# Three matmul operands at other places in SBUF: the mixer's output, the gates' second operand, the values' activations

## The chip, the core and the metric

The kernel runs on one core of one Trainium2 chip. The metric is the device time of the program on that core in microseconds (us). The time of a kernel is the median of its runs.

## What is computed

One layer of an encoder over 256 tokens (`S`) of width 2048 (`D`), all in float32. Cut to what matters here:

```
mod = silu(c) @ w_ada + b_ada            # six vectors: shift, scale, gate, twice
h   = x * (1 + scale1) + shift1
mix = concat([ssd(h @ w_in), shortconv(h @ w_in)]) @ w_out     # 4096 columns of mixer output
x   = layer_norm(alpha * x + gate1 * mix)
h   = x * (1 + scale2) + shift2
q   = h @ w_query                        # 8 heads, product keys, top 16 of 128*128 experts
act = gelu(expert_u @ h) * gate          # 16384 experts as 128 chunks of 128
x   = layer_norm(alpha * x + gate2 * (act @ expert_v))
```

## The kernel before

Everything runs with features or experts on the 128 partitions. Weights stream in as blocks of 128x1024 floats (`raw`), and `wsplit` (L70 to L83) cuts each into a high and a low part, `hi` on ACT (L78) and `lo` on DVE (L81). A product is then three matmuls with float32r operands, written in `mm3` (L91 to L93): high weight with high activation, high with low, low with high. A matmul here has two operands in SBUF: the **weight** (the stationary one, 128 columns, loaded by an LDWEIGHTS ahead of it) and the **moving** one, which streams through. PE runs them in the order in which the program issues them; the profile shows the loads as the engine PEld.

In order of time, the stages and their matmuls are:

- `ps` and `ps_b` (`unit_b`), then `ps_in` (`inproj`): the input projection. The moving operand is `h2h` or `h2l`, 256 columns; the weight is `hi` or `lo`.
- `ps_o` (the loop over `d0, d1` after `out_chunk`): the output projection. The moving operand is the mixer's output, tiles `y` (`y_tiles`, L224 to L226; written in `rms` by `split`, L118 to L120). 3 x 512 = 1536 matmuls of 256 columns.
- `ps_q`: the queries, moving `h2h` and `h2l` again, and the top-16 search on DVE.
- `ps_u` (`act_chunk`, L821 to L826): the 128 chunks of `expert_u`, 48 matmuls each, moving `h2h` and `h2l`. In the first 64 chunks `proj` calls `step` twice a chunk, and each call puts one pair of **gate matmuls** (`ps_g`, L814, in `gates`) between two groups of 24 matmuls of `ps_u`. Their weight is `eq` (a comparison result of DVE, L803), their moving operand is `o2`, which ACT writes (L809). The results `ge` of these chunks go out to HBM (`gel_d`, L841) and come back in the second 64 chunks (L849).
- `ps_v` (`mm_v`, L874 to L881): act @ expert_v. Here the roles turn: the weight is the activation, `ah` or `al` (`a_pair`, L867 to L872), and the moving operand is the split block of `expert_v`, `hi` or `lo`, 512 columns. 3 x (992 + 32) = 3072 matmuls.

Which tile lies where in SBUF is set by the pools: tiles of a pool stand in the order in which they are first asked for, one after the other, and a pool that is opened with `side="right"` grows from the other end. The tiles of the change are in the pools `prm` (with `scb`, `par`, and ahead of `yp`, which holds `y`), `wk4a` (`eq`, `o2`, `ge`) and `wk5` (right side: `big5`, `g2b`, `st`, `ah`, `al`). The order of instructions is the program's own with some priorities; the change touches none of them.

Of the kernel before, what the change touches and what calls it, by code (L numbers as in the profile page):

```python
# [7 lines left out]
F32 = mybir.dt.float32  # L8
F32R = mybir.dt.float32r
# [9 lines left out]
P = 128  # L19
S = 256  # L20
D = 2048
ND = D // P
NE = 128
# [17 lines left out]
def layer_kernel(ctx, tc, I, out, dbg=None):  # L41
    nc = tc.nc
# [6 lines left out]
    def pool(stack, name, bufs=1, **kw):  # L49
        return stack.enter_context(tc.tile_pool(name=name, bufs=bufs, reuse_waits="tile", **kw))  # L50
# [169 lines left out]
    prm = pool(st2, "prm")  # L220
# [7 lines left out]
    scb = prm.tile([P, D], F32, name="scb")  # L228
    par = prm.tile([P, 194], F32, name="par")
    at = 0  # L230
# [564 lines left out]
    with ExitStack() as p4:  # L795
# [3 lines left out]
        def gates(q):  # L799

            eq = wk.tile([P, 2, 2, NE], F32R, name="eq", tag="eq")
            t0 = 2 * q
# [17 lines left out]

        def act_chunk(e2, wk, n, beside=None):  # L821
            ps = pu.tile([P, S], F32, name="ps_u", tag="pu")
            proj([ps], [I["expert_u"][e2]], *h2, ND, beside=beside)
            ge = wk.tile([P, S], F32, name="ge", tag="ge", bufs=n)
            other(ge, ps, AF.Gelu)
            return ge  # L826

        with ExitStack() as p4a:
            wk = pool(p4a, "wk4a", 2)
            pairs = (g for q in range(S // 2) for g in (gates(q),))  # L830
            g = next(pairs)
            next(g)

            def step():
                nonlocal g
                next(g, None)
                g = next(pairs, iter(()))
                next(g, None)

            for e2 in range(STAGE):  # L840
                nc.sync.dma_start(gel_d[e2], act_chunk(e2, wk, 1, step))  # L841
        wk = pool(p4, "wk4b")
# [13 lines left out]
    with ExitStack() as p5:  # L856
# [7 lines left out]
        g2b = wk.tile([P, D], F32, name="g2b")  # L864
        st = wk.tile([P, 2, 16], F32, name="st")

# [7 lines left out]
        def mm_v(tb, c, ah, al, vh, vl, lo, start, stop):  # L874

            ts = slice(tb * P, (tb + 1) * P)
            if not lo:
                T.matmul(banks[tb][c], ah[:, ts], vh, start=start, stop=False)  # L878
                T.matmul(banks[tb][c], al[:, ts], vh, start=False, stop=False)  # L879
            else:  # L880
                T.matmul(banks[tb][c], ah[:, ts], vl, start=False, stop=stop)  # L881


# [14 lines left out]
        for e2 in range(NE - LAST):  # L898
            if e2 % 2 == 0:
                ah, al = a_pair(e2)  # L900
            if e2 == FIRST:
# [133 lines left out]
```

## Time and profile before

| what | value |
|---|---|
| median of 3 runs | 2547.92 us |
| the 3 runs | 2544.36, 2547.92, 2559.14 us |
| the profiled execution, its own time | 2552.61 us |
| its span in the trace, first to last instruction | 2550.7 us |
| PE busy | 2424.6 us, 95% |
| DVE busy, ACT busy | 1862.2 us (73%), 1381.3 us (54%) |
| mean granted clock of PE | 0.984 |

The page's busy share of PE says that some matmul is in flight. It does not say how far apart they start. Matmuls overlap in the trace: a matmul of 256 columns is shown 0.28 us long, but the next one starts some 0.11 us after it. So the pace of PE is read from starts in the timeline, or from the number of matmuls in a stretch without waits. In a window the count also takes in two matmuls that began before the window's edge.

### The profile page before, as it was taken

Reading aid. Unit: us, or ns where it says so; the run is one execution under the profiler, and the core shown is the slowest. Engines: PE = TensorE matmul, PEld = TensorE weight load, DVE = VectorE, ACT = ScalarE, POOL = GpSimd, SP = SyncE. Lnnn points to the kernel's source line nnn. Section 1 sums busy time; section 2 is a strip of 40 time slices with the busy share of each in tenths; the row PEclk is TensorE's granted clock in tenths of the full one; section 3 lists DMA queues with packets and bytes.
Section 4 is the critical chain, followed back from the end, with each engine's and each line's share of the span. In section 5 each row is a group of like instructions: output and inputs, shape, how many; then the busy total and the mean of one; then the engine's idle time right before and its main releaser. Section 6 shows DMA issues by size and latency. Waiting matters only on the chain.

```text
span 2550.7 us, 44290 instructions
## 1 busy us (share of the span) xinstructions
PE 2424.6 (95%) x17122; PEld 2248.3 (88%) x17122; DVE 1862.2 (73%) x3255; ACT 1381.3 (54%) x2506; POOL 0.9 (0%) x7
## 2 busy tenths in 40 slices
PE   5889999999999899999999999999998999999997
PEld 5889888888899799999999999999886888888886
DVE  8788888989887799898888855555675555645545
ACT  3435476656444554499999944444443444544442
POOL 0000000000000000000000000000000000000000
PEclk9999999999999899999999999999999999999999
DMA  9886766778887565355666666666788655655554
GB/s 356 313 297 236 260 217 224 235 260 280 267 291 259 196 206 181 116 181 193 199 195 200 198 218 219 218 217 219 257 307 274 217 194 190 223 192 193 193 190 149
DMA packets 183252, 575.67 MB, mean 226 GB/s; under 512 B 22209, under 2 KB 44929, under 8 KB 182657
## 3 DMA queue, kind: packets, MB, share of 16 engines
q1 hardware_dynamic: 183042, 572.85, 67.3%
q8 instruction: 134, 2.20, 0.3%
q14 instruction: 76, 0.62, 0.1%
HBM read 560.10 MB, written 12.66 MB: 225 GB/s over the span
## 4 chain that ended last, share of the span: by engine, by line
PE 67%; DMA 15%; DVE 12%; ACT 3%; issue 2%; SPq 1%; DVEq 0%; ACTq 0%
PE ps_u L91 9%; PE ps_u L92 9%; PE ps_u L93 9%; PE ps_v L879 8%; PE ps_v L881 8%; PE ps_v L878 8%; DVE lo L81 5%; DMA adaw<-in_w_ada_dram 4%; DMA raw<-in_w_in_dram 3%; DMA big<-in_w_ada_dram 2%; ACT hi L78 2%; DVE adaw L152 2%; DMA raw<-in_w_inA_dram 2%; PE ps_q L93 2%; PE ps_q L92 2%
## 5 line engine op out<-in xcount | busy, mean ns | idle before, releaser
L81 DVE TENSOR_TENSOR lo<-raw,hi 128x1024 fp32r<-128x1024 f32 (+1 forms) x804 | 972.1, 1212 | 506.8 <-ACT hi L78 504.7
L78 ACT ACTIVATE hi<-raw 128x1024 fp32r<-128x1024 f32 (+1 forms) x804 | 843.6, 1051 | 884.6 <-PE ps_v L879 302.1
L91 PE MATMUL ps_u<-h2h,hi 128*128 128x256 f32 x2048 | 568.7, 278 | 0.0
L92 PE MATMUL ps_u<-h2l,hi 128*128 128x256 f32 x2048 | 568.1, 277 | 0.0
L93 PE MATMUL ps_u<-h2h,lo 128*128 128x256 f32 x2048 | 568.1, 277 | 0.0
L878 PE MATMUL ps_v<-hi,ah 128*128 128x512 f32 x992 | 390.1, 393 | 9.9 <-ACT hi L78 8.1
L879 PE MATMUL ps_v<-hi,al 128*128 128x512 f32 x992 | 390.7, 394 | 1.2 <-DVE al L120 1.2
L91 PEld LDWEIGHTS ps_u<-h2h,hi 128*128 128x128 f32 x2048 | 386.2, 189 | 0.0
L92 PEld LDWEIGHTS ps_u<-h2l,hi 128*128 128x128 f32 x2048 | 384.6, 188 | 0.0
L93 PEld LDWEIGHTS ps_u<-h2h,lo 128*128 128x128 f32 x2048 | 384.5, 188 | 0.0
L881 PE MATMUL ps_v<-lo,ah 128*128 128x512 f32 x992 | 268.9, 393 | 0.8 <-DVE lo L81 0.8
L878 PEld LDWEIGHTS ps_v<-hi,ah 128*128 128x128 f32 x992 | 187.5, 189 | 52.3 <-ACT hi L78 8.9
L879 PEld LDWEIGHTS ps_v<-hi,al 128*128 128x128 f32 x992 | 187.7, 189 | 43.0 <-DVE al L120 1.6
L91 PE MATMUL ps_in<-h2h,hi 128*128 128x256 f32 x768 | 222.3, 289 | 3.0 <-DVE mod L159 2.2
L881 PEld LDWEIGHTS ps_v<-lo,ah 128*128 128x128 f32 x992 | 186.8, 189 | 42.0 <-DVE lo L81 2.0
L93 PE MATMUL ps_in<-h2h,lo 128*128 128x256 f32 x768 | 217.6, 283 | 2.3 <-DVE lo L81 2.3
L152 DVE SCALAR_TENSOR_TENSOR adaw<-adaw,scb 128x1024 f32<-128x1024 f32 x160 | 193.1, 1219 | 35.3 <-DMA adaw<-in_w_ada_dram 35.0
L92 PE MATMUL ps_in<-h2l,hi 128*128 128x256 f32 x768 | 217.6, 283 | 0.0
L809 ACT ACTIVATE o<-eq,gT 128x128 fp32r<-128x128 f32 x512 | 161.4, 388 | 0.0
L91 PEld LDWEIGHTS ps_in<-h2h,hi 128*128 128x128 f32 x768 | 146.6, 191 | 9.0 <-issue 4.2
L93 PEld LDWEIGHTS ps_in<-h2h,lo 128*128 128x128 f32 x768 | 147.1, 191 | 4.6 <-DVE lo L81 2.9
L93 PE MATMUL ps_o<-y,lo 128*128 128x256 f32 x512 | 145.6, 284 | 5.0 <-DVE lo L81 4.9
(285 smaller groups left out, 3975.0 us busy)
## 6 DMA issues: line engine op xcount, KB each, us to landing
raw<-in_expert_u_dram SPq DMA_DIRECT2D x256, 512.0 KB, 4.5
raw<-in_expert_v_dram SPq DMA_DIRECT2D x248, 512.0 KB, 3.9
adaw<-in_w_ada_dram SPq DMA_DIRECT2D x160, 512.0 KB, 6.0
raw<-in_w_in_dram SPq DMA_DIRECT2D x110, 512.0 KB, 5.0
raw<-in_w_out_dram SPq DMA_DIRECT2D x64, 512.0 KB, 4.3
raw<-in_w_query_dram SPq DMA_DIRECT2D x64, 512.0 KB, 3.9
raw<-in_w_inB_dram SPq DMA_DIRECT2D x44, 512.0 KB, 4.4
big<-in_w_ada_dram SPq DMA_DIRECT2D x32, 512.0 KB, 5.6
```

The lines of the kernel that those rows point to most:

```text
L78: A.activation(hi, raw, AF.Copy)
L81: V.tensor_tensor(lo, raw, hi.bitcast(F32), op=ALU.subtract)
L91: T.matmul(ps, wh, mh, start=start, stop=False)
L92: T.matmul(ps, wh, ml, start=False, stop=False)
L93: T.matmul(ps, wl, mh, start=False, stop=stop)
L152: V.scalar_tensor_tensor(w, w, 0.5, scb[:, cs], op0=ALU.mult, op1=ALU.mult, accum_out=macc[:, half, part % 2, d:d + 1])
L809: A.activation(o2[:, k], eq[:, i, 1].bitcast(F32), AF.Copy, scale=gT[:, k, t0 + i:t0 + i + 1])
L878: T.matmul(banks[tb][c], ah[:, ts], vh, start=start, stop=False)
L879: T.matmul(banks[tb][c], al[:, ts], vh, start=False, stop=False)
L881: T.matmul(banks[tb][c], ah[:, ts], vl, start=False, stop=stop)
```

## The change

Three tiles are asked for in another order or with some padding, so that they, and what stands behind them in their pools, start elsewhere. Nothing is computed otherwise. In the built programs each engine has the same instructions in the same order with the same waits; only start addresses differ, and the row length of the three padded tiles (`par`, `ge`, `st`). No row of the order moves, so none is shown.

```diff
-    par = prm.tile([P, 194], F32, name="par")
+    par = prm.tile([P, 226], F32, name="par")[:, :194]
...
         def gates(q):
-            eq = wk.tile([P, 2, 2, NE], F32R, name="eq", tag="eq")
+            eq = wk.tile([P, 2, 2, NE], F32R, name="eq", tag="eq") if q else eq0
...
-        def act_chunk(e2, wk, n, beside=None):
+        def act_chunk(e2, wk, n, beside=None, ge=None):
...
-            ge = wk.tile([P, S], F32, name="ge", tag="ge", bufs=n)
+            ge = wk.tile([P, S], F32, name="ge", tag="ge", bufs=n) if ge is None else ge
...
         with ExitStack() as p4a:
             wk = pool(p4a, "wk4a", 2)
+            ge = lambda: wk.tile([P, S + 48], F32, name="ge", tag="ge", bufs=1)[:, :S]
+            eq0 = wk.tile([P, 2, 2, NE], F32R, name="eq", tag="eq")
+            ge0 = ge()
...
-                nc.sync.dma_start(gel_d[e2], act_chunk(e2, wk, 1, step))
+                nc.sync.dma_start(gel_d[e2], act_chunk(e2, wk, 1, step, ge() if e2 else ge0))
...
         g2b = wk.tile([P, D], F32, name="g2b")
-        st = wk.tile([P, 2, 16], F32, name="st")
...
+        a_first = a_pair(0)
+        st = wk.tile([P, 2, 24], F32, name="st")
...
             if e2 % 2 == 0:
-                ah, al = a_pair(e2)
+                ah, al = a_pair(e2) if e2 else a_first
```

Where the operands stand, from the two built programs. The numbers in the last four columns are the start within its partition, taken modulo 256 bytes; all buffers of a tile, and all parts of it that a matmul reads, have the same remainder.

| matmuls | columns | count | moving, before | weight, before | moving, after | weight, after |
|---|---|---|---|---|---|---|
| `ps`, `ps_b`, `ps_in`, `ps_q`, `ps_u` | 256 | 11616 | 224 | 32 | 224 | 32 |
| `ps_o` (moving `y`) | 256 | 1536 | 96 | 32 | 224 | 32 |
| `ps_g` (moving `o2`) | 256 | 256 | 32 | 32 | 224 | 32 |
| `ps_v` (weight `ah`, `al`) | 512 | 3072 | 32 | 224 | 32 | 32 |

In bytes, `y` goes from 100192 to 100320 and on, `o2` from 193312 to 194528 (1216 further, 1024 of which is `ge`, now in front of it), and `ah` from 217056 to 216864. All that stands behind `par` in `prm` and all later pools of that side up to the end of the mixer go 128 bytes further too: scratch of DVE and ACT, `h2w`, `xsT`, `Emat`. `big5` and `g2b` go 64 bytes lower. `hi`, `lo`, `raw`, `h2h`, `h2l`, `eq` and `GA` stay.

## Rows read from the trace of the kernel before

**Rows 1.** The page: busy time of each engine, share of the span, instructions.

```profile
PE 2424.6 (95%) x17122; PEld 2248.3 (88%) x17122; DVE 1862.2 (73%) x3255; ACT 1381.3 (54%) x2506; POOL 0.9 (0%) x7
```

**Rows 2.** Windows by stage: stretch, us, busy time and count per engine, clock, DMA, GB/s.

```profile
657.00:852.00 195.00, 186.56 (x1531) 183.86 (x1530) 146.46 (x243) 81.48 (x107) 0.24 (x1) 0.98 0.80 266
1158.00:1466.00 308.00, 308.00 (x2659) 308.00 (x2659) 260.48 (x409) 287.46 (x770) 0.00 (x0) 1.00 0.62 198
1466.00:1816.00 350.00, 349.64 (x3085) 349.44 (x3083) 201.03 (x259) 154.94 (x198) 0.00 (x0) 1.00 0.68 218
1816.00:2550.70 734.70, 709.39 (x3072) 579.79 (x3072) 409.29 (x448) 309.78 (x340) 0.00 (x0) 0.98 0.65 215
```

**Rows 3.** Windows without a wait of PE, in ps_o, ps_u and ps_v.

```profile
815.00:850.00 35.00, 35.00 (x299) 35.00 (x299) 19.92 (x25) 15.67 (x19) 0.24 (x1) 1.00 0.61 192
1500.00:1800.00 300.00, 300.00 (x2650) 300.00 (x2649) 171.59 (x220) 132.38 (x166) 0.00 (x0) 1.00 0.68 218
1990.00:2530.00 540.00, 540.00 (x2361) 443.07 (x2360) 278.29 (x268) 236.85 (x254) 0.00 (x0) 1.00 0.59 194
```

**Rows 4.** Timeline of PE at two gate pairs: start us, length us, instruction.

```profile
1231.32 0.28 PE L91 MATMUL ps_u<-h2h,hi 128*128 128x256 f32 x1
...
1231.91 0.28 PE L93 MATMUL ps_u<-h2h,lo 128*128 128x256 f32 x1
1232.03 0.40 PE L814 MATMUL ps_g<-o,eq 128*128 128x256 f32 x2
1232.27 0.28 PE L91 MATMUL ps_u<-h2h,hi 128*128 128x256 f32 x1
...
1232.62 0.28 PE L91 MATMUL ps_u<-h2h,hi 128*128 128x256 f32 x1
...
1233.19 0.28 PE L93 MATMUL ps_u<-h2h,lo 128*128 128x256 f32 x1
...
1235.00 0.39 PE L814 MATMUL ps_g<-o,eq 128*128 128x256 f32 x2
1235.23 0.28 PE L91 MATMUL ps_u<-h2h,hi 128*128 128x256 f32 x1
1235.35 0.28 PE L92 MATMUL ps_u<-h2l,hi 128*128 128x256 f32 x1
...
1235.94 0.28 PE L91 MATMUL ps_u<-h2h,hi 128*128 128x256 f32 x1
```

**Rows 5.** Timeline of PE after the first and the last of 31 stalls.

```profile
27.66 0.28 PE L93 MATMUL ps<-h2h,lo 128*128 128x256 f32 x1
27.96 0.38 PE L91 MATMUL ps<-h2h,hi 128*128 128x256 f32 x1
...
31.00 0.28 PE L93 MATMUL ps<-h2h,lo 128*128 128x256 f32 x1
31.68 0.28 PE L93 MATMUL ps<-h2h,lo 128*128 128x256 f32 x1
...
877.39 0.28 PE L92 MATMUL ps_q<-h2l,hi 128*128 128x256 f32 x1
879.64 0.45 PE L93 MATMUL ps_q<-h2h,lo 128*128 128x256 f32 x1 [1.97 <-DVE lo L81]
...
883.99 0.28 PE L91 MATMUL ps_q<-h2h,hi 128*128 128x256 f32 x1
884.70 0.28 PE L91 MATMUL ps_q<-h2h,hi 128*128 128x256 f32 x1
```

**Rows 6.** One window with waits of PE, in ps_o.

```profile
733.00:800.00 67.00, 62.93 (x515) 61.01 (x514) 53.40 (x92) 26.53 (x33) 0.00 (x0) 1.00 0.86 294
```

**Rows 7.** Groups of DVE by form, operands at 96, 32 and 224: busy us, mean ns.

```profile
L120 DVE TENSOR_TENSOR y<-xsC,y 128x256 fp32r<-128x256 f32 x16 | 5.8, 415 | 0.0
L845 DVE TENSOR_TENSOR GA<-GA,ge 128x256 f32<-128x256 f32 x64 | 26.7, 417 | 0.0
L185 DVE TENSOR_TENSOR rT<-rT,ln_s 128x256 f32<-128x256 f32 x16 | 6.6, 420 | 0.2
```

## The prediction

> **What bounds the kernel.** I read the page first: PE is busy 95% of the span, DVE 73%, ACT 54% [rows 1]. Then the windows by stage: in the gate stage and the rest of ps_u PE has no gap, and in ps_o and ps_v little [rows 2]. So the pace of matmuls sets the time, and the reader has to look at how far apart they start, which a busy share does not tell. Three windows without a wait, all at a granted clock of 1.00, the 2.4 GHz level, give it; I take off the two matmuls that began before each window [rows 3]. In ps_o 297 matmuls take 35 us, 117.8 ns each. In ps_u 2648 take 300 us, 113.3 ns. In ps_v 2359 take 540 us, 228.9 ns. At one column a cycle, 256 columns are 106.7 ns and 512 are 213.3 ns. So the excess over the columns is 11.1 ns in ps_o, 6.6 ns in ps_u and 15.6 ns in ps_v: three levels, some 4.45 ns apart. No engine is late in these windows, and ps_o and ps_u are the same instruction with the same kind of weight. What differs is where the moving operand stands: 96 in ps_o, 224 in ps_u (all places modulo 256 bytes).
>
> Place is not all of it. At gate pairs the timeline shows ps_u, with unmoved places, at both paces [rows 4]. From 1231.32 to 1231.91 five matmuls are 118 ns apart; after the gate pair at 1232.03 they are 114 ns apart (1232.62 to 1233.19); after the next pair, at 1235.00, 118 ns again (1235.35 to 1235.94). So at 224/32 (moving/weight) two paces exist, call them **fast** and **slow**. PE keeps the one it has, and a gate pair, at 32/32, turns it over. That goes on through the stage: it averages 308 us for 2657 matmuls, 115.9 ns, the middle of both paces, while the second half of ps_u runs at 349.64/3083 = 113.4 ns [rows 2]. A stall draws the pace anew. Of the 31 places where PE stood over 150 ns with only 224/32 matmuls around, the first at 27.66 us and the last at 877.39, 20 go on fast and 11 slow; the first settles at 113.3 ns (0.68 us for six), the last at 118.3 ns (0.71 us for six) [rows 5]. At 96/32, in ps_o, no stall is followed by the fast pace.
>
> **The change, part by part.**
>
> *Values (ps_v), 32/224 to 32/32.* No row shows 512 columns at 32/32. Bounds: the least excess seen, 6.6 ns, would make it 220.0 ns, 3072 x 8.9 = 27.3 us less; one step of 4.45 ns above today's would make it 233.3 ns, 13.7 us more. The nearest row is the gate pair itself, 32/32 with 256 columns: 0.24 us for two out of the slow pace, 0.23 us out of the fast one [rows 4], so 120 and 115 ns, mean 117.5, an excess of 10.8. The nearest of the three levels is 11.1. I take 213.3 + 11.1 = 224.4 ns: 3072 x 4.45 = **13.7 us less**. It lies on the path: DVE is busy 409 us and ACT 310 us of 735 us there [rows 2].
>
> *Mixer's output (ps_o), 96/32 to 224/32.* The places become those of ps_u, so the fast pace becomes possible. If held throughout, it saves 1536 x 4.45 = 6.8 us; the other bound is 0. PE stalls often here, and each stall draws again. Between 733 and 800 us the 513 matmuls need 60.4 us of 67, and the DMA queues are at 0.86 [rows 6]; there a faster PE waits longer for the same blocks, so I count nothing. The other 1023 save 4.45 ns in 20 of 31 cases: **3.0 us less**.
>
> *Gates (ps_g), 32/32 to 224/32.* The pair becomes like its neighbours, so it should no longer turn the pace over. The stage then keeps the pace that the last stall ahead of 1158 us left. If fast, 2657 x 113.3 ns = 301.0 us instead of 308: **7.0 us less**. ACT, busy 287.5 us of these 308 [rows 2], still fits into 301 and is late next. If slow, see the first rival.
>
> *The rest.* Scratch of DVE and ACT moves by 128 or 64 bytes. DVE takes 415 ns for 128x256 with operands at 96, 417 at 32 and 420 at 224 [rows 7], so I cost it at nothing; behind PE it would have cover in any case. The order, the waits and the DMAs are the same in both programs, and no engine gets an instruction more.
>
> Sum: 13.7 + 3.0 + 7.0 = 23.7 us less. The profiled execution took 2552.6 us, 4.7 above the median of the three runs; it would become 2528.9, and the median of runs 2547.9 - 23.7 = **2524 us**. The three runs lie 15 us apart, about what 3083 matmuls at one pace or the other cost (13.6 us), so I expect such a spread after the change as well.
>
> **Rivals.**
>
> 1. *The slow pace is locked in (slower).* Today gate pairs turn the pace over 128 times, so the stage pays half. Without them a slow draw at the last stall, near 1158 us, stays until ps_u ends at 1816: there is no wait of PE in between [rows 2]. Price: 2657 x 117.8 = 313.0 instead of 308 us, and 3083 x 117.8 = 363.2 instead of 349.6: +18.6 us, with ps_o still 3.0 less. For it: 11 of 31 stalls end slow. Against it: 20 do not. It decides against the change once ps_v saves under 15.6 us. With ps_v at 224.4 ns it gives +1.9, 2550 us; with ps_v unchanged +15.6, 2563 us.
>
> 2. *ps_v keeps 228.9 ns.* Then the level there goes with 512 columns or with the moving operand at 32, and not with the weight's place. For it: the gate pair has never been a steady stream. Then 3.0 + 7.0 = 10.0 less, 2538 us, in the fast case.
>
> 3. *ps_v drops to 220.0 ns*, since a weight at 32 is what all fast matmuls have: 27.3 + 10.0 = 37.3 less, 2511 us; with rival 1, 11.7 less, 2536 us. Its mirror, a step up to 233.3 ns, gives +3.7, 2552 us, or with rival 1 +29.3, 2577 us.
>
> 4. *Places do nothing*, and ps_o and ps_v are slower for a reason of their own: 2548 us. Against it: the same instruction runs in ps_o and ps_u at two levels, and ps_o never reaches the fast one after a stall. The Trainium skill speaks for this rival: the page TensorE: Matmul & The Clock Gate, section Step-by-step: what each phase is for, says that weights and moving data come through two independent read ports, so that loading the next weights takes nothing from the running matmul. By that rule no place would matter and the sum would be 0. The trace does not bear it out: the excess here has three levels that this rule does not explain.
>
> **How the numbers follow.** Chances: the forecast 0.29; ps_v at 224.4 with a slow lock 0.14; ps_v unchanged, fast 0.15 and slow 0.07; ps_v at 220.0, fast 0.14 and slow 0.06; ps_v worse, fast 0.05 and slow 0.03; no effect of places 0.07. A measurement can tell about 0.5%, 12.7 us. Over 12.7 us faster are the forecast and the fast case at 220.0, and parts of those at 2536 and 2538: 0.51. Over 12.7 us slower are 2563 and 2577 and a part of the case at 2550: 0.12. The rest is 0.37. The range goes from below the 2511 case to above the 2550 and 2552 ones, 2508 to 2556, which leaves out the two cases beyond. The forecast's own range, with ps_o between 0 and 6.8, is 2520 to 2527.
>
> **What would show it.** Right: 512-column starts of ps_v 224.4 ns apart in 1990 to 2530; ps_o at 113.3 ns in most stretches; no change of pace at gate pairs, and one pace from about 1158 to 1816 us. Wrong: gate pairs that still turn the pace over; ps_o at 117.8 ns after every stall; ps_v at 228.9 ns or more. The slow lock would show as 117.8 ns through the second half of ps_u.

## The result, and the profile after

The change made the kernel slower. Its median is 2567.11 us (2560.84 to 2570.51, 6 runs) against 2550.64 us of the kernel before (2544.36 to 2559.14, 6 runs), a ratio of 1.0061 with a 95% interval from 1.0037 to 1.0084. The forecast was 2524 us and its range 2508 to 2556, so the result lies outside. All six runs lie above all six of before. In the later comparisons single runs of before reach higher (about a quarter of 96 are above 2560.84 us), so it takes the whole set of runs to tell the two kernels apart. The profiled execution of after took 2565.29 us, its span is 2563.2 us.

The page of after, busy time of each engine, answers to [rows 1]:

```profile
PE 2433.6 (95%) x17122; PEld 2261.3 (88%) x17122; DVE 1867.0 (73%) x3255; ACT 1386.2 (54%) x2506; POOL 0.9 (0%) x7
```

Nothing shows there: each share is what it was. As before, the windows must be read by their counts. First the stages of ps_u in after, then its windows without a wait, in the columns of [rows 2, 3]:

```profile
1158.00:1182.00 24.00, 24.00 (x213) 24.00 (x212) 20.32 (x34) 21.85 (x62) 0.00 (x0) 1.00 0.60 197
1182.00:1466.00 284.00, 284.00 (x2414) 284.00 (x2413) 241.10 (x373) 266.06 (x698) 0.00 (x0) 1.00 0.61 195
1466.00:1822.00 356.00, 356.00 (x3025) 356.00 (x3024) 196.92 (x254) 153.69 (x201) 0.00 (x0) 1.00 0.66 210
...
815.00:850.00 35.00, 35.00 (x299) 35.00 (x299) 19.52 (x25) 15.57 (x18) 0.24 (x1) 1.00 0.62 193
1500.00:1800.00 300.00, 300.00 (x2549) 300.00 (x2549) 165.84 (x213) 126.73 (x160) 0.00 (x0) 1.00 0.66 210
2040.00:2530.00 490.00, 490.00 (x2164) 405.73 (x2163) 252.13 (x229) 218.99 (x230) 0.00 (x0) 1.00 0.63 198
```

Two matmuls come off each count, as in the prediction. From 1158 to 1182 us 211 matmuls take 24 us, 113.7 ns each: PE comes into the gate stage fast. From 1182 to 1466 us it is 284/2412 = 117.7 ns, and in the second half of ps_u 300/2547 = 117.8 ns, where before had 113.3 [rows 3]. So the slow pace is locked in from about 1182 us to the end of ps_u, although PE came in fast. ps_v is at 490/2162 = 226.6 ns, between the 228.9 of before and the 224.4 of the forecast. ps_o is at 117.8 ns in its window here, but not always, as the runs below show.

Where the lock begins is in the timeline of after, PE, around two gate pairs (start us, length us, instruction):

```profile
1181.67 0.28 PE L91 MATMUL ps_u<-h2h,hi 128*128 128x256 f32 x1
...
1182.35 0.42 PE L814 MATMUL ps_g<-o,eq 128*128 128x256 f32 x2
...
1183.30 0.28 PE L91 MATMUL ps_u<-h2h,hi 128*128 128x256 f32 x1
...
1185.00 0.28 PE L91 MATMUL ps_u<-h2h,hi 128*128 128x256 f32 x1
...
1185.34 0.41 PE L814 MATMUL ps_g<-o,eq 128*128 128x256 f32 x2
...
1186.06 0.28 PE L92 MATMUL ps_u<-h2l,hi 128*128 128x256 f32 x1
...
1188.06 0.28 PE L91 MATMUL ps_u<-h2h,hi 128*128 128x256 f32 x1
...
1188.41 0.40 PE L814 MATMUL ps_g<-o,eq 128*128 128x256 f32 x2
```

Ahead of the pair at 1182.35, from 1181.67, six starts take 0.68 us, 113 ns each. After it PE goes on fast: 1183.30 to 1185.00 is 15 steps of 113 ns. After the pair at 1185.34 it is slow: 1186.06 to 1188.06 is 17 steps of 118 ns, and so it stays. What differs is the length of the pairs: 0.42 and 0.41 us instead of the 0.39 to 0.40 of a pair that runs through [rows 4]. What makes them longer stands in the same timeline with all engines, once at a fast pair and once at a slow one:

```profile
1175.11 1.25 ACT L809 ACTIVATE o<-eq,gT 128x128 fp32r<-128x128 f32 x4
...
1176.27 0.33 PEld L814 LDWEIGHTS ps_g<-o,eq 128*128 128x128 f32 x2
...
1176.76 0.40 ACT L818 ACTIVATE GA<-ps_g 128x124 f32<-128x124 f32 x1 [0.40 <-DVE GA L819]
...
1468.87 0.69 ACT L809 ACTIVATE o<-eq,gT 128x128 fp32r<-128x128 f32 x2
...
1470.02 0.30 PEld L814 LDWEIGHTS ps_g<-o,eq 128*128 128x128 f32 x2
```

At the fast pace ACT finishes o2 at 1175.11 + 1.25 = 1176.36 us, after the first gate matmul's load began at 1176.27. The pair of loads takes 0.33 us instead of 0.30: the second one is **held**. At the slow pace ACT is done at 1469.56 and the loads begin 0.46 us later, so nothing is held. One gate pair with its 24 matmuls of ps_u takes PE 26 x 113.3 ns = 2.946 us fast and 26 x 117.8 = 3.063 us slow. The held pairs start at 1176.38, 1179.37, 1182.35 and 1185.34, 2.99 us apart: that is ACT's period, between the two. ACT's work in a pair is less, 266.06 us in 2412/26 = 92.8 pairs, 2.87 us, but it also waits for DVE, 0.40 us in the row above.

So the theory to test, **A**: the pace is kept until something disturbs it; a hold of PE at a gate pair draws the pace anew; a pair at 224/32 by itself leaves it alone. PE is held only at the fast pace, so slow is where it ends up in every run, and nothing after the last pair brings it back. Rivals: **B**, the pair at 224/32 itself turns fast into slow; **C**, no draw at all, ACT's work or another moved tile slows PE. (The recorded expectations of the first four runs use B and C for rivals of their own.)

### The profile page after: what moved, and what is told of

Same layout as the page of the kernel before. It is cut to its first block, busy times and chain, and to the rows that moved or that the text cites. A ratio compares the mean times of both kernels' runs of the same rounds, so it can differ in the third digit from the quotient of the medians.

```text
span 2563.2 us, 44290 instructions
## 1 busy us (share of the span) xinstructions
PE 2433.6 (95%) x17122; PEld 2261.3 (88%) x17122; DVE 1867.0 (73%) x3255; ACT 1386.2 (54%) x2506; POOL 0.9 (0%) x7
## 4 chain that ended last, share of the span: by engine, by line
PE 66%; DMA 15%; DVE 12%; ACT 3%; issue 2%; SPq 1%; DVEq 0%; ACTq 0%
PE ps_u L92 9%; PE ps_u L93 9%; PE ps_u L91 9%; PE ps_v L882 7%; PE ps_v L881 7%; PE ps_v L884 7%; DVE lo L81 5%; DMA adaw<-in_w_ada_dram 4%; DMA raw<-in_w_in_dram 3%; DMA big<-in_w_ada_dram 3%; DVE adaw L152 2%; ACT hi L78 2%; PE ps_q L93 2%; PE ps_q L92 2%; PE ps_q L91 2%
## 5 line engine op out<-in xcount | busy, mean ns | idle before, releaser
L91 PE MATMUL ps_u<-h2h,hi 128*128 128x256 f32 x2048 | 575.0, 281 | 0.0
L93 PE MATMUL ps_u<-h2h,lo 128*128 128x256 f32 x2048 | 574.6, 281 | 0.0
L92 PE MATMUL ps_u<-h2l,hi 128*128 128x256 f32 x2048 | 574.5, 281 | 0.0
```

The costliest lines, as they stand in the source:

```text
L91: T.matmul(ps, wh, mh, start=start, stop=False)
L92: T.matmul(ps, wh, ml, start=False, stop=False)
L93: T.matmul(ps, wl, mh, start=False, stop=stop)
```

## The experiments

Each kernel is compared with runs of the kernel before on the same chip; the medians of before in these comparisons go from 2548.36 to 2558.22 us. The columns on the right are counts of matmuls in two windows of the profiled execution, 1182:1466 and 1500:1800, as they stand in the trace. The ratios are those on record for the two sets of runs; they need not be the quotients of the two medians.

| kernel | median us (range, runs) | ratio to before, 95% interval | 1182:1466 | 1500:1800 |
|---|---|---|---|---|
| before | 2550.64 (2544.36 to 2559.14, 6) | | 2452 | 2650 |
| after | 2567.11 (2560.84 to 2570.51, 6) | 1.0061, 1.0037 to 1.0084 | 2414 | 2549 |
| mixer's output alone | 2557.89 (2545.99 to 2572.16, 12) | 0.9985, 0.9955 to 1.0015 | 2452 | 2549 |
| values alone | 2547.98 (2539.19 to 2567.06, 12) | 0.9963, 0.9932 to 0.9994 | 2454 | 2649 |
| gates alone | 2570.06 (2557.32 to 2580.59, 12) | 1.0040, 1.0012 to 1.0069 | 2414 | 2550 |
| after, one 32/32 pair at half | 2549.44 (2545.69 to 2560.76, 12) | 0.9979, 0.9952 to 1.0006 | 2417 | 2650 |
| after, ACT's copies left out | 2540.47 (2530.22 to 2567.26, 10) | 0.9979, 0.9945 to 1.0013 | 2509 | 2650 |
| after, o2 further ahead | 2553.37 (2545.46 to 2568.07, 12) | 0.9999, 0.9982 to 1.0016 | 2380 | 2550 |
| after, half of o2 on DVE | 2578.22 (2569.39 to 2582.76, 6) | 1.0112, 1.0094 to 1.0131 | 2332 | 2649 |
| after, gates at 160/32 | 2540.67 (2534.93 to 2545.91, 9) | 0.9944, 0.9922 to 0.9965 | 2473 | 2649 |
| after, stream at 212/32 | 2602.39 (2586.06 to 2604.50, 6) | 1.0175, 1.0144 to 1.0206 | 2342 | 2435 |
| after, gates at 224/160 | 2541.90 (2534.15 to 2546.20, 8) | 0.9924, 0.9897 to 0.9951 | 2472 | 2650 |

The two kernels not in the table run matmuls alone.

### The parts one by one

Mixer's output alone:

```diff
-    par = prm.tile([P, 194], F32, name="par")
+    par = prm.tile([P, 226], F32, name="par")[:, :194]
```

> The kernel before with the mixer's output alone 128 bytes further (y from 96 to 224, modulo 256 bytes). Theory A (a matmul whose operands stand at 224/32 has two paces, 113.3 and 117.8 ns, and draws one after each stall; at 96/32 it has the slow one alone): ps_o shows both paces, some 40 to 65% of its stretches fast, and the time falls by 2 to 4 us, within what can be told from no change. Rival B (the moved places are bad in themselves and cost time in every part): ps_o does not speed up and the time rises by a third of the 16 us.

Values alone:

```diff
-        st = wk.tile([P, 2, 16], F32, name="st")
...
+        a_first = a_pair(0)
+        st = wk.tile([P, 2, 24], F32, name="st")
...
-                ah, al = a_pair(e2)
+                ah, al = a_pair(e2) if e2 else a_first
```

> The kernel before with the values' activations alone 192 bytes lower (ah, al from 224 to 32). Theory A: ps_v goes from 228.9 to 226.7 ns a matmul, 3072 x 2.2 = 6.8 us less; ps_u is as in the kernel before, with a pace that turns over at each gate pair. About 2544 us against 2551. Rival B: ps_u turns slow here too, and the time rises.

Gates alone is the rest of the change:

```diff
-            eq = wk.tile([P, 2, 2, NE], F32R, name="eq", tag="eq")
+            eq = wk.tile([P, 2, 2, NE], F32R, name="eq", tag="eq") if q else eq0
...
+            ge = lambda: wk.tile([P, S + 48], F32, name="ge", tag="ge", bufs=1)[:, :S]
+            eq0 = wk.tile([P, 2, 2, NE], F32R, name="eq", tag="eq")
+            ge0 = ge()
```

> The kernel before with the gates' second operand alone 192 bytes further (o2 from 32 to 224). Theory A (at the fast pace PE catches up with ACT and is held a few tens of ns at the second matmul of a gate pair; each hold draws the pace anew, until it is slow; the slow pace is not held and so stays to the end of ps_u): the gate stage at 117.8 ns for most of it and the second half of ps_u wholly at 117.8 ns; 5 to 5.5 us more in the one and 13.6 us more in the other than the profiled execution before, so 2565 to 2572 us in all runs. Rival C (the pace in ps_u is drawn once a run, by chance): about half of the runs near 2545 us, half near 2568.

The gates carry the loss: alone they are at 2570.06 us, by the medians 15 us over the 2554.69 us that before had in this comparison (ratio 1.0040). The twelve runs go from 2557.32 to 2580.59 us, none near 2545, so this run's own rival, one draw a run, falls. The windows are those of after:

```profile
1182.00:1466.00 284.00, 284.00 (x2414) 284.00 (x2413) 241.13 (x372) 266.56 (x699) 0.00 (x0) 1.00 0.61 194
1500.00:1800.00 300.00, 300.00 (x2550) 300.00 (x2549) 165.82 (x214) 126.69 (x160) 0.00 (x0) 1.00 0.66 210
```

The values bring a gain, 0.9963, and its interval holds the 6.8 us (a ratio of 0.9973) that 226.67 instead of 228.9 ns make in 3072 matmuls. Of the mixer's output the time tells nothing, the interval holds 1. Its profile does tell something. Here are its gate stage and its second half:

```profile
1182.00:1466.00 284.00, 284.00 (x2452) 284.00 (x2452) 239.11 (x376) 264.42 (x702) 0.00 (x0) 1.00 0.63 198
1500.00:1800.00 300.00, 300.00 (x2549) 300.00 (x2548) 165.87 (x213) 126.67 (x159) 0.00 (x0) 1.00 0.66 210
```

In this kernel the gate pairs stand as before and turn the pace over each time, so the stage has the count of before, 2452. But the second half is slow, where the profile of before had it fast. With pairs that turn the pace over, the second half depends on the side on which the last pair leaves it, and that is 13.6 us between two runs of one kernel. That would make the greater part of the 15 us spread of before's first six runs, though only the profiled ones show their pace, and it hides what ps_o gains.

What ps_o gains is itself less plain than the profile of before made it. In values alone and gates alone `y` was not moved, ps_o is at 96/32, and yet stretches of it run fast. Here is one in gates alone, behind a stall of 1.62 us:

```profile
780.90 0.28 PE L91 MATMUL ps_o<-y,hi 128*128 128x256 f32 x1
...
791.56 0.28 PE L92 MATMUL ps_o<-y,hi 128*128 128x256 f32 x1
```

These are 94 steps in 10.66 us, 113.4 ns each. Of the distances at one of the two paces, 10% are fast in the ps_o of values alone and 18% in that of gates alone, under 1% in before. So 96/32 has the fast pace too, which the prediction took to be absent there. With `y` at 224 the share goes from 37% to 90% in eight profiles: the fast pace comes up more often, but it is not new.

With `y` moves `h2w`, the moving operand of 112 plain float32 products of ps_in, from 96 to 224 as well; its matmuls are 216.7 ns apart in before and in after, so it plays no part.

### Is it the pace that is kept, or the work around it?

The change, with one pair of matmuls more at 32/32 behind the first group of chunk 64, thus after all gate pairs; weight and moving operand are pieces of a tile `hi` that is there anyway:

```diff
+                for i in range(2):
+                    T.matmul(pt[:, i].rearrange("p k e -> p (k e)"), w[:, :P], w[:, :S], start=True, stop=True)
...
-            ge = act_chunk(e2, wk, 2)
+            ge = act_chunk(e2, wk, 2, flip)
```

> The changed kernel plus one pair of matmuls with both operands at 32 (the places that the gate pair had before), put once behind the first 24 matmuls of the second half of ps_u; their result is not used. Theory A: the pair turns the locked slow pace over, the rest of the second half runs at 113.3 ns, 3050 x 4.45 = 13.6 us less than the changed kernel: 2553 to 2556 us. Rival B: the second half stays at 117.8 ns and the time at 2567 us.

Its timeline, PE, around the added pair (`ps_f`):

```profile
1466.10 0.28 PE L95 MATMUL ps_u<-h2l,hi 128*128 128x256 f32 x1
...
1467.98 0.28 PE L96 MATMUL ps_u<-h2h,lo 128*128 128x256 f32 x1
1468.10 0.40 PE L858 MATMUL ps_f<-hi 128*128 128x256 f32 x2
...
1468.69 0.28 PE L94 MATMUL ps_u<-h2h,hi 128*128 128x256 f32 x1
1468.80 0.28 PE L95 MATMUL ps_u<-h2l,hi 128*128 128x256 f32 x1
1468.92 0.28 PE L96 MATMUL ps_u<-h2h,lo 128*128 128x256 f32 x1
```

Ahead of the pair 16 steps take 1.88 us, 118 ns; behind it they take 0.11 to 0.12 us, and the second half then has 2648 matmuls in 300 us, 113.3 ns. Two matmuls in 0.24 us win back the second half: 2549.44 us, some 18 us under after. Nothing was done to ACT or DVE, so C falls for the second half: the slow pace there is a state that PE was left in.

The next three kernels ask what puts PE into it. In the first, ACT's copy out of the gates' PSUM is left out:

```diff
-                A.activation(o, pt[:, :, 0, cs], AF.Copy)
-                V.tensor_tensor(o, o, pt[:, :, 1, cs], op=ALU.add)
+                V.tensor_copy(o, pt[:, :, 1, cs])
```

> This kernel is the change, but leaves out ACT's copy of the first of the two gate products and the addition to it (DVE copies the second product alone), so ACT has some 0.7 us less to do for each gate pair and has o2 ready long before PE asks for it. Theory A (the slow pace was locked in because PE, at the fast pace, is held 20 to 40 ns at a gate pair by ACT's o2, and a hold draws the pace anew; at the slow pace there is no hold): without holds the pace with which PE comes to 1158 us stays, 113.3 ns with 301 and 349 us for the two stages if it comes fast, as it did in the profile of the change (then about 2541 us in all), 117.8 ns if it comes slow (then about 2567 us). Theory B (a gate pair at 224/32 turns fast into slow by itself and never back): slow from the first few gate pairs on, whatever PE came with, 313 and 363 us, and about 2567 us.

Its windows, with the one in ps_o ahead:

```profile
815.00:850.00 35.00, 35.00 (x311) 34.95 (x309) 20.67 (x25) 15.39 (x18) 0.24 (x1) 1.00 0.63 203
1182.00:1466.00 284.00, 284.00 (x2509) 284.00 (x2507) 216.38 (x377) 223.50 (x514) 0.00 (x0) 1.00 0.63 203
1500.00:1800.00 300.00, 300.00 (x2650) 300.00 (x2649) 172.13 (x222) 132.23 (x166) 0.00 (x0) 1.00 0.68 218
```

The gate pairs stand at 224/32 as in after, and through the whole stage the pace is 284/2507 = 113.3 ns. So the pair does not turn fast into slow, and B falls. The ten runs fall into heaps, as A expects where the pace of arrival is kept: five from 2530.22 to 2536.84 us, four from 2556.48 to 2567.26, one at 2544.10. The first window shows that ps_o at 224/32 can be fast as well, 35/309 = 113.3 ns.

In the second, the operands o2 are prepared a step earlier, in the same room:

```diff
+                V.tensor_tensor(o2[:, 1], iota, eT[:, t0 + i, 1:2].to_broadcast([P, NE]), op=ALU.is_equal)
                 for k in range(2):
-                    A.activation(o2[:, k], eq[:, i, 1].bitcast(F32), AF.Copy, scale=gT[:, k, t0 + i:t0 + i + 1])
+                    A.activation(o2[:, k], o2[:, 1].bitcast(F32), AF.Copy, scale=gT[:, k, t0 + i:t0 + i + 1])
...
             prepare()
+            prepare()
```

> This kernel is the change with the gate operands made one step further ahead: DVE writes the comparison that o2 is made from into o2 itself, so that with the same room there are four o2 tiles instead of two, at the same places modulo 256, and ACT and DVE prepare a gate pair two calls of step before PE uses it. DVE has two instructions of 128 columns a pair more (about 0.2 us of 2.7 us). Theory A (holds at gate pairs draw the pace): PE is never held for o2, so the pace that PE brings to 1158 us stays up to 1816 us: fast gives 301 and 349 us and about 2541 us, slow 313 and 363 us and about 2567 us; over the runs a mixture of these two, with a median that depends on how often PE comes fast. Theory B (the gate pair itself turns fast into slow): always slow, 2567 us. If ACT and DVE are still late for another reason, holds remain and the result is that of the change, 2567 us.

Its gate stage, and one of its gate pairs (L815 here) with ACT's o2 (L810), each from its own view:

```profile
1182.00:1466.00 284.00, 284.00 (x2380) 278.89 (x2380) 241.89 (x547) 250.97 (x683) 0.00 (x0) 1.00 0.60 191
```

```profile
1251.44 1.30 ACT L810 ACTIVATE o<-o,gT 128x128 fp32r<-128x128 f32 x4
...
1252.51 0.46 PEld L815 LDWEIGHTS ps_g<-o,eq 128*128 128x128 f32 x2
...
1252.62 0.55 PE L815 MATMUL ps_g<-o,eq 128*128 128x256 f32 x2
```

This missed its aim. PE is held at most pairs, here by 0.16 us (0.46 instead of 0.30), and a pair with its group takes 284 x 26/2378 = 3.105 us, more than even the slow pace needs. The second load begins, 0.19 us ahead of the end of the two, at 1252.78, when ACT's o2 is done at 1252.74. So the lead is used up: ACT and DVE, which now hand over once for every o2 instead of once a pair, need longer than PE (that it is these handovers is my reading, no run separates it), and preparing earlier does not help an engine that is late by its period. But A's middle part shows: between the held pairs both paces come up all through the stage (some two thirds of the distances in it that are at one of the two paces are fast), no pace locks in, and the second half is whatever the last hold left. The runs are spread from 2545.46 to 2568.07 us.

Whether a hold really draws is open. I take as a hold's length what it adds to the 340 ns from the last start of ps_u ahead of a pair to the first behind it. In the profiles of after, gates alone and the kernel with one 32/32 pair, the three holds that ended the fast pace were 16, 17 and 19 ns long; the 16 that kept it were 8, 10 or 22 to 35 ns long. With o2 further ahead, 16 holds out of the fast pace ended slow and 45 fast, and no length, to the ns, was on both sides. So the length of a hold may settle what I call a draw. No run sets that length on purpose; for the account here it is enough that sooner or later a hold ends slow.

In the third, DVE takes half of the o2 products from ACT:

```diff
-                for k in range(2):
-                    A.activation(o2[:, k], eq[:, i, 1].bitcast(F32), AF.Copy, scale=gT[:, k, t0 + i:t0 + i + 1])
+                A.activation(o2[:, 0], eq[:, i, 1].bitcast(F32), AF.Copy, scale=gT[:, 0, t0 + i:t0 + i + 1])
+                V.tensor_scalar(o2[:, 1], eq[:, i, 1].bitcast(F32), gT[:, 1, t0 + i:t0 + i + 1], None, op0=ALU.mult)
```

> This kernel is the change with half of the work on o2 moved from ACT to DVE: of the four products a gate pair that make o2, ACT keeps the two of the high part and DVE makes the two of the low part. ACT has some 0.6 us less to do a gate pair, DVE some 0.4 us more (about 2.4 of 2.95 us). The program's scheduler then puts some of the second gate matmuls a few matmuls later. Theory A (ACT's chain of work for a gate pair takes longer than the 2.95 us that PE needs for 26 matmuls at the fast pace, so PE is held there, each hold draws the pace anew, and the slow pace, 3.06 us, is without holds and stays): with ACT's chain shorter there are no holds, so the pace with which PE comes to 1158 us stays to 1816 us, and the runs fall into two heaps, about 2540 us (fast) and about 2567 us (slow), as with ACT's copies left out; the median depends on how many come fast, six in ten by the share of fast matmuls ahead of 1158 us. Theory C (it was not the holds but ACT's work itself or its traffic in SBUF that slows PE, and leaving it out helped for that reason): a shift of all runs together by a part of what leaving the copies out gave, no two heaps.

```profile
1158.00:1182.00 24.00, 22.91 (x178) 21.18 (x178) 23.11 (x51) 18.06 (x46) 0.00 (x0) 1.00 0.50 158
1182.00:1466.00 284.00, 284.00 (x2332) 274.97 (x2331) 260.50 (x537) 192.59 (x494) 0.00 (x0) 1.00 0.59 188
...
1500.00:1800.00 300.00, 300.00 (x2649) 300.00 (x2648) 171.65 (x220) 132.27 (x166) 0.00 (x0) 1.00 0.68 218
```

A miss as well, and the expectation of both theories fell. ACT has room now, 192.59 of 284 us, but DVE, 260.50 of 284, is late in its place: the view of PE's waits, from 1100 to 1900 us (us in total, times, longest), has it as the one that holds the gates in the longest waits.

```profile
PE ps_g L814 <- DVE o L809: 2.5, 9, 0.3
```

The stage runs at 284/2330 = 121.9 ns a matmul, and the time is 2578.22 us. The run does not tell A from C; it shows that the fast pace leaves neither ACT nor DVE much to give.

### The paces, measured by themselves

A kernel with matmuls alone, the operands at the 64 pairs of places:

```diff
+            T.matmul(ps[:, :n], wt[:, g:g + P], mt[:, f:f + n], start=k == 0, stop=k == len(places) - 1)
...
+    for m in range(8):
+        for w in range(8):
+            for r in range(4):
+                batch([(m, w)] * 30, 256)
```

> This kernel leaves out the whole layer: it runs batches of float32r matmuls alone, the moving and the weight operand each at the 8 places 0, 32, ... 224 modulo 256, 256 columns in 4 batches of 30 and 512 columns in 2 of 24 for each of the 64 pairs of places, a copy out of the single PSUM buffer between batches, so that PE stands ahead of each batch. Then batches of 12 matmuls at 224/32 (moving/weight), with one or with two matmuls at one of the 64 pairs of places put between the twelves, three times a batch. Theory A (pace depends on the places, and where two paces exist PE keeps the one it has): 256 columns are 113.3 or 117.8 ns at 224/32, and both come up among the batches; 117.8 ns in all batches at 96/32; 512 columns 226.7 ns at 32/32 and about 228.9 ns at 32/224; two matmuls at 32/32 between twelves at 224/32 turn the pace over each time (113, 118, 113 or the reverse), two more at 224/32 never do. Rival (places do nothing, the other work of the layer makes the paces): one pace in all batches of one width and no change of pace within a batch.

The pace of a steady stream is the mean distance of the last 16 (256 columns) or 12 (512 columns) starts of each batch, the very first batch left out. It depended only on the **difference** of the two places, weight minus moving, modulo 256; the eight pairs of one difference agreed within 0.2 ns, unless a range stands here:

| weight minus moving | 0 | 32 | 64 | 96 | 128 | 160 | 192 | 224 |
|---|---|---|---|---|---|---|---|---|
| 256 columns, ns | 120.0 | 118.3 | 113.3 or 117.8 | 117.2 to 120.0 | 118.6 to 118.9 | 120.0 | 117.8 | 116.7, rarely 117.8 |
| 512 columns, ns | 226.7 | 233.3 | 233.3 | 233.8 to 234.6 | 231.7 to 233.3 | 233.3 | 228.9 | 233.3 |

This is the ground of the change. ps_u and its like stand at a difference of 64, ps_o stood at 192 (117.8) and went to 64, ps_v stood at 192 (228.9) and went to 0 (226.7, the best of its row). With nothing of the layer around, the same numbers come out, so the rival "places do nothing" is excluded. The Trainium skill's rule of two independent read ports (TensorE: Matmul & The Clock Gate, section Step-by-step: what each phase is for), by which loading weights takes nothing from the running matmul, would by itself make all entries of a row equal; here they go from 113.3 to 120.0 ns, and the measurement decides. In these batches the same stream has two paces at a difference of 64, now and then at 224, and several at 96. At 192 all 32 batches are at 117.8 ns, while ps_o at 192 also ran at 113.4 ns in gates alone: the batches, with one tile for all weights and one for all moving operands, do not show every pace that the layer has.

A second kernel puts one or two matmuls at each pair of places between twelves at 224/32, in the order of `mm3`, once as it comes and once behind a 32/32 pair:

```diff
+                    if turn:
+                        ops += [other(1, 1, i) for i in range(2)] + [base(k) for k in range(12)]
+                    for r in range(3):
+                        ops += [other(m, w, i) for i in range(n)] + [base(k) for k in range(12)]
```

> This kernel leaves out the whole layer: batches of matmuls of 256 columns at 224/32 (moving/weight) in the order of mm3 (hi with h2h, hi with h2l, lo with h2h), twelve at a time, with one or two matmuls at one of the 64 pairs of places modulo 256 between the twelves, each once as it comes and once with a 32/32 pair ahead that should turn the pace over; then 24 matmuls with the weight's place moved in steps of 4 bytes. Theory A: a pair at 32/32 turns the pace over from either side, a pair at 224/32 from neither; among the other places are some that lead from slow to fast and keep fast. Only the difference weight minus moving modulo 256 sets the pace of a steady stream, 113.3 or 117.8 ns at 64; between the steps of 32 bytes nothing is known: steps of 4 bytes may all be slower, or some may be fast without a slow twin. Rival (an insertion does nothing of its own, the pace is drawn at every change of weights): the 32/32 pair keeps or turns the pace about equally often.

One batch in its timeline: twelve at 224/32, a 32/32 pair at 1756.26, twelve, a 160/32 pair at 1757.90, twelve, another at 1759.50 (both kinds read `mt` and `wt`):

```profile
1755.58 0.28 PE L69 MATMUL ps<-h2h,hi 128*128 128x256 f32 x1
...
1756.15 0.28 PE L69 MATMUL ps<-h2h,lo 128*128 128x256 f32 x1
1756.26 0.39 PE L69 MATMUL ps<-mt,wt 128*128 128x256 f32 x2
...
1756.84 0.28 PE L69 MATMUL ps<-h2h,hi 128*128 128x256 f32 x1
...
1757.79 0.28 PE L69 MATMUL ps<-h2h,lo 128*128 128x256 f32 x1
1757.90 0.40 PE L69 MATMUL ps<-mt,wt 128*128 128x256 f32 x2
...
1758.25 0.28 PE L69 MATMUL ps<-h2l,hi 128*128 128x256 f32 x1
...
1759.39 0.28 PE L69 MATMUL ps<-h2h,lo 128*128 128x256 f32 x1
1759.50 0.40 PE L69 MATMUL ps<-mt,wt 128*128 128x256 f32 x2
```

Before the 32/32 pair 5 steps take 0.57 us (114 ns), behind it 8 take 0.95 us (119 ns), behind the 160/32 pair 10 take 1.14 us (114 ns). Over the whole kernel, with F and S for the pace of each twelve: 32/32 pairs gave F S F S from fast and went on F S F S F when turned first; 224/32 pairs gave F F F F, and F S S S S when turned first; 160/32 pairs gave F F F F, and F S F F F. The 32/32 pair put first turned the pace over in all 128 batches that have one. So an inserted pair is no draw. At these places it acted the same way each time: 32/32 turns the pace over, 224/32 keeps it, 160/32 brings it to fast from either side. For the 32/32 pair this confirms the reading of [rows 4], and for the 224/32 pair it excludes B once more. The rival of this run, that a 32/32 pair keeps the pace as often as it turns it, falls.

### Versions built on this

Gates at 160/32, the change with 64 bytes less behind ge:

```diff
-            ge = lambda: wk.tile([P, S + 48], F32, name="ge", tag="ge", bufs=1)[:, :S]
+            ge = lambda: wk.tile([P, S + 32], F32, name="ge", tag="ge", bufs=1)[:, :S]
```

> This kernel is the change with 16 floats less of padding behind ge, so that o2 stands at 160 instead of 224 modulo 256 and a gate pair is at 160/32; nothing else moves. In the batches of matmuls alone, a pair at 160/32 between twelves at 224/32 led from slow to fast and kept fast, and cost some 15 ns more than a pair at 224/32 (355 instead of 340 ns for three starts). Theory A (the pace is kept unless a pair at other places or a hold changes it): whatever a hold of PE by ACT's o2 does, the next gate pair brings the fast pace back, so most of the gate stage is fast (302 to 306 us instead of 313), the last pair leaves the second half of ps_u fast in every run (350 instead of 363 us), and the runs come to about 2545 us, with a spread of some 10 us; no run above 2560 us. Theory C (what ACT does slows PE, and the places of the pair matter only by their own cost): the second half stays slow as in the change, about 2567 us.

```profile
1182.00:1466.00 284.00, 284.00 (x2473) 284.00 (x2472) 239.15 (x380) 258.25 (x713) 0.00 (x0) 1.00 0.63 199
1466.00:1816.00 350.00, 347.67 (x3063) 346.96 (x3061) 201.81 (x260) 155.49 (x198) 0.00 (x0) 1.00 0.68 219
1500.00:1800.00 300.00, 300.00 (x2649) 300.00 (x2648) 171.95 (x222) 132.33 (x166) 0.00 (x0) 1.00 0.68 218
```

The second half is fast, 300/2647 = 113.3 ns, and the gate stage does 2471 matmuls where after does 2412. 2540.67 us is 10 to 14 us under before and 26 under after, and the nine runs lie within 11 us, none above 2546. It came out some 4 us better than expected. In its trace the first distances behind a pair are 116, 120, 114, 124 and 118 ns, then 113, at nearly every pair, just as in the matmuls alone; with the distances of the pair itself that makes 40 ns more than 14 matmuls at 113.3. Twice, behind the pairs at 1252 and 1458 us, a group came out slow, and the next pair made it fast again. ACT has the same instructions in a pair as in after, so C falls for the gate stage too.

The whole stream 12 bytes lower, where steps of 4 bytes in the second kernel of matmuls had shown 113.3 ns twice:

```diff
-    h2h = h2p.tile([P, ND, S], F32R, name="h2h")
-    h2l = h2p.tile([P, ND, S], F32R, name="h2l")
+    h2b = h2p.tile([P, 2 * ND * S + 8], F32R, name="h2b")[:, 5:5 + 2 * ND * S]
+    h2h, h2l = (h2b[:, i * ND * S:(i + 1) * ND * S].rearrange("p (d t) -> p d t", d=ND) for i in range(2))
...
-    par = prm.tile([P, 226], F32, name="par")[:, :194]
+    par = prm.tile([P, 218], F32, name="par")[:, :194]
...
-            ge = lambda: wk.tile([P, S + 48], F32, name="ge", tag="ge", bufs=1)[:, :S]
+            ge = lambda: wk.tile([P, S + 32], F32, name="ge", tag="ge", bufs=1)[:, :S]
```

> This kernel is the change with h2h and h2l in one tile and 12 bytes lower, at 212 instead of 224 modulo 256, so that all matmuls of the input projection, the queries and ps_u are at 212/32, a difference of 76 bytes, where the batches alone showed 113.3 ns after both stalls (2 of 2; at a difference of 64 it was 117.7 and 113.3). To make room y goes to 192, which puts ps_o at 192/32, and o2 to 160. If a difference of 76 has no slow twin, all these streams run at 113.3 ns after every stall: the second half of ps_u 350 us, the gate stage 302 to 306 us, and in the input projection and the queries, where some four in ten of 5472 matmuls were slow, up to 4.45 x 0.4 x 5472 = 10 us less, a part of which the DMA queues take back; ps_o stays at 117 ns or gets slower (up to 120 ns, 3 us). Then about 2540 us, from 2533 to 2547. If it has a slow twin too, its runs of slow matmuls show after stalls at 117 to 120 ns, and the time is 2555 to 2575 us.

```profile
1500.00:1800.00 300.00, 300.00 (x2435) 300.00 (x2434) 158.89 (x204) 120.63 (x151) 0.00 (x0) 1.00 0.63 201
```

A clear miss: 300/2433 = 123.3 ns, and 2602.39 us. The batches had all weights in one tile and all moving operands in another; in the layer they alternate between tiles. Whether that makes the difference stays open; two batches were too few to build on.

Last, gates at 224/160, the pair that led to fast in the batches and cost nothing of its own:

```diff
-            ge = lambda: wk.tile([P, S + 48], F32, name="ge", tag="ge", bufs=1)[:, :S]
+            ge = lambda: wk.tile([P, S + 32], F32, name="ge", tag="ge", bufs=1)[:, :S]
+            ge0 = ge()
             eq0 = wk.tile([P, 2, 2, NE], F32R, name="eq", tag="eq")
-            ge0 = ge()
+            wk.tile([P, 16], F32, name="pad", tag="pad", bufs=1)
```

> This kernel is the change with ge in front and 16 floats between eq and o2, so that eq stands at 160 instead of 32 and a gate pair is at 224/160; all streams stay. In the batches alone a pair at 224/160 led from slow to fast, kept fast, and cost nothing beside its two matmuls (three starts in 340 ns), where the pair at 160/32 cost 40 ns more with its after-effects. Theory A with ACT as the limit (at the fast pace PE needs 26 x 113.3 = 2.946 us for a gate pair with its group, and ACT about 2.98 us): PE runs into ACT's o2 again, the second load of a pair is held by up to 40 ns, some holds turn the pace to slow for one group and the next pair turns it back; the gate stage takes as long as with the pair at 160/32, whose own 40 ns a pair filled that gap, the second half of ps_u is fast in every run, and the time is 2540 us, give or take 4. If ACT can follow, 128 x 40 ns = 5 us less, 2535 us. If the second half comes out slow in some runs, a hold after the last pair or the pair itself doesn't do what the batches showed, and runs above 2552 us come up.

```profile
1182.00:1466.00 284.00, 284.00 (x2472) 283.83 (x2472) 239.14 (x378) 257.56 (x711) 0.00 (x0) 1.00 0.63 199
...
1500.00:1800.00 300.00, 300.00 (x2650) 300.00 (x2649) 172.05 (x221) 131.65 (x165) 0.00 (x0) 1.00 0.69 218
```

2541.90 us and the same count in the gate stage, 2472 against 2473: 284 x 26/2470 = 2.99 us a pair. Its timeline at one pair:

```profile
1200.97 1.25 ACT L809 ACTIVATE o<-eq,gT 128x128 fp32r<-128x128 f32 x4
...
1202.13 0.33 PEld L814 LDWEIGHTS ps_g<-o,eq 128*128 128x128 f32 x2
```

The two loads take 0.33 us again, with ACT's o2 done at 1200.97 + 1.25 = 1202.22: PE runs into ACT and is held, some groups come out slow, and a later pair mends them. ACT is busy 257.56 us of the 284, in 2470/26 = 95.0 pairs 2.71 us each; the other 0.28 us of each it is idle, for the most part behind DVE. So ACT's period, 2.99 us a pair, is the floor of this stage, as expected, and the 40 ns of the pair at 160/32 only filled the gap. Both versions beat the kernel before and the change; between the two the runs show no difference.

## Why the prediction was wrong

**The reading of the kernel** held in the main. The pace of starts sets the time, it goes by the places, two paces exist at 224/32, and a 32/32 pair turns one into the other. The rival "places do nothing" fell. One reading did not hold: "at 96/32, in ps_o, no stall is followed by the fast pace" was true of one profile, and two others of the same places have fast stretches.

**Values: right in direction, mis-sized.** The term said 224.4 ns and 13.7 us less. It measured 226.6 to 226.7 ns, so 6.8 us. The step that failed is the nearest row: the gate pair, 32/32 with 256 columns, seen between other matmuls. A steady stream at a difference of 0 has 120.0 ns with 256 columns, the worst of its row together with 160, and 226.7 with 512, the best of its row. Excess over the columns does not carry from one width to the other, and the levels are more than three.

**Mixer's output: not to be told in the time.** Both paces come up in ps_o (fast 40% of the distances at one of the two paces in after, 90% in the kernel with this part alone, 45% in the one with gates at 160/32). But the premise that only the move makes the fast pace possible was wrong: unmoved, the share was under 1%, 10% and 18%. The share of 20 in 31 taken for the moved one stands for no run in particular. From its first to its last start ps_o took 198.5 us in after and 196.3 in before, so between these two profiles it won nothing, and the 3.0 us are within what hides in 13.6 us of spread.

**Gates: the wrong side.** The forecast had 7.0 us less and gave the slow lock a chance of three in ten, after 11 slow stalls of 31. The mechanism and the price of this rival were right: 18.6 us was its price, and the windows give (2452 - 2414) x 117.7 ns = 4.5 us in the stage and 3083 x 4.45 ns = 13.7 us in the second half, 18.2 together. Two steps failed. The first is "the stage then keeps the pace that the last stall ahead of 1158 us left". It does so only where nothing disturbs PE, as the kernel without ACT's copies shows; in after PE came in fast and lost it within 30 us. The second is "ACT, busy 287.5 us of these 308, still fits into 301 and is late next". Busy time fits. But 2657/26 = 102 pairs in 308 us make 2.81 us of work a pair, PE at the fast pace asks for one every 2.946 us, and ACT waits for DVE as well. Where PE runs into it all through the stage, with the gates at 224/160, ACT has 2.71 us of work and 0.28 us idle a pair: its period is 2.99 us. So PE catches up with ACT and is held, again and again, until a hold leaves it slow, and at the slow pace it is never held. Slow was not one outcome of two but the only one that lasts. A chance near one was called for.

Between the two profiled executions the stages add up, each from its first to its last start: ps_u took 761.6 us instead of 743.9, ps_v 714.6 instead of 719.1 (its pace alone would give 6.8 us less), all ahead of ps_u 1.0 us less, and the end 0.3 us more. These are the 12.5 us between the spans of 2550.7 and 2563.2 us. The medians lie 16.5 us apart. Where pairs turn the pace over, the second half of before can end fast, as in its profile, or slow, as in the kernel with the mixer's output alone, and the medians of before in the six comparisons go from 2548.36 to 2558.22 us; so I leave the other 4 us of that difference open.

## What to carry to other kernels

When an edit takes away something that disturbs a rhythm, ask which state lasts, not which is likelier: a state in which nothing waits is kept, one that runs into a neighbour is lost. An engine fits under a faster one by its period, waits included, per unit of work, and not by its busy share of the stage. And where a matmul stream is back to back, read the distance of starts against the places of both operands: moving a small operand of a neighbour can cost or give 4% of the stream.

## What was not expected of the hardware

- With nothing else running, the distance of starts of 256-column float32r matmuls went from 113.3 to 120.0 ns with the difference of the two operands' places modulo 256, and that of 512 columns from 226.7 to 234.6, in another order. The best difference for one width, 64, is among the poor ones for the other (233.3), and the best for 512 columns, 0, is with 160 the worst for 256.
- At a difference of 64 the same stream runs at 113.3 or 117.8 ns (in the layer at 192 too, in ps_o) and stays there for hundreds of microseconds, 3083 matmuls in the second half of ps_u, until a hold or a matmul at other places changes it.
- What an inserted pair does went by its places: 32/32 turns over, 224/32 keeps, 160/32 and 224/160 lead to fast. Behind a 160/32 pair the same five distances, 116, 120, 114, 124 and 118 ns, come in the layer and in the matmuls alone. What in the chip makes it so, no run here tells.
- A hold of PE of some tens of ns can end with another pace: in after behind one of 16 ns the slow pace came and stayed, behind ones of 22 to 35 ns the fast one went on.
- Places between the steps of 32 bytes have paces of their own, and what 24 matmuls showed of them, 113.3 ns at 76, was 123.3 ns in the layer.
